# A streaming encoder step on one core: the first projection's rows are divided by their rms beforehand, and its results leave PSUM in fewer steps

## The chip, the core and the metric

The kernel runs on one core of a Trainium2 chip. TensorE (PE) multiplies matrices into PSUM, VectorE (DVE), ScalarE (ACT) and GpSimd (POOL) do the elementwise work, and SyncE (SP) issues the transfers. The metric is the device time of one execution in microseconds (us), the median of several runs. Each engine works through its own list of instructions strictly in order; that list is fixed when the program is built.

## The reference

One layer of a hybrid encoder runs over 2048 prompt rows and 32 sample rows of 1024 features. What the change touches is the first norm and the first projection, and what is made of its columns:

```python
def rmsnorm(x, g):
    y = x32 * lax.rsqrt(jnp.mean(x32 * x32, axis=-1, keepdims=True) + NORM_EPS)
    return (y * g.astype(jnp.float32)).astype(x.dtype)
...
z = RMSNorm(x) @ w_in        # q, k, v (768 columns) and the RWKV part zr (1792 columns)
z_prev = jnp.concatenate([shift_prev.astype(zr.dtype), zr[:, :-1]], axis=1)
zs = zr + (z_prev - zr) * lw['rwkv_mu']
r, k, v, wd, ad, gd = jnp.split(zs, RWKV_SPLITS, axis=-1)
```

q, k and v go to a sliding-window attention, zs to an RWKV-7 recurrence over chunks of 64 rows. Their outputs are joined and projected (w_out), a cross attention over 256 memory rows follows, then a feed-forward block with squared relu and a last norm. Besides y, the last projected row (the shift) and caches are returned.

## The kernel before

Everything is held transposed: features on the 128 partitions, rows of the sequence along the free axis. Products are made in three passes for accuracy: an operand w is split into a high part w_h and a rest w_l (ACT writes the high part, DVE or POOL subtracts for the rest), x likewise into xh and xl, and `mm3` (L230, its matmuls on lines 234, 235 and 236) adds xh w_h + xl w_h + xh w_l over eight slices of 128 features: 24 matmuls, called a group below.

The 2080 rows form four groups of rows (0 to 3) of 544, 512, 512 and 512, each cut into two blocks of 272 or 256. For group of rows g, phase Yg projects the 14 units of 128 columns that make zr, phase Zg the 6 units of q, k, v. Each unit's weights are loaded once and used for both blocks, so the groups on PE alternate between first and second block. `prep` (L264) makes a block ready: it loads x to `xb`, of which there is one buffer, writes xh (ACT, with the norm's gain as its scale) and xl (DVE, `gsplit`), and returns a function for the row norms. That function (`rms`, L193, with `sumsq`, L176) squares each slice on ACT, adds the squares on POOL (for rows 0 to 543 PE adds them instead), sums over partitions by a matmul with ones, `ps_rms` (L190), and makes 1/rms by two activations, Ln and Exp. It is called behind the first group's matmuls. So PE multiplies rows that aren't divided yet, and the division is part of the evacuation of `ps_z`: DVE multiplies by `rms_acc` from PSUM to `zo` (for q with 0.125 too). For zr there follow two steps on `zo`: ACT writes mu times `zo`, shifted by one row, to `zm`; DVE adds omu times `zo` (omu is 1 - mu) and `zm`, in place. SP then stores `zo` to zrw or zqkv in memory, from where the RWKV tiles (`zin`, L528) and the attention tiles load it. `ps_z` and `ps_rms` share two PSUM banks (`pmm`, L81); a bank is free for the next group once its reader is done. `zo` and `zm` have three buffers each, the weights two.

A list written by hand (PLAN, L35) names the phases in order: Y0 and Z0, then 17 RWKV tiles (R00 to R33 and Rs), attention tiles (A), Y1 to Z3, the output projection (O), cross attention (C, X, D), and then the feed-forward part. From it, from priorities for each kind of work (the recurrence's first, the matmuls of `mm3` last, as fillers) and from modelled durations, a scheduler fixes every engine's list. The RWKV tiles are one long chain in which each tile needs the state of the one before; groups of `mm3` fill PE in between.

Of the kernel before, what the change touches and what calls it, by code (L numbers as in the profile page):

```python
# [22 lines left out]
KC = D // P  # L23
# [27 lines left out]
def hymba_step_kernel(  # L51
# [46 lines left out]
    def pc(key, i, n=1):  # L98
        return par[:, PG[key] + i:PG[key] + i + n]
# [161 lines left out]
    def halves_of(g):  # L261
        return [(0, 272), (272, 272)] if g == 0 else [(0, 256), (256, 256)]

    def prep(src, nb, gkey, nk=KC, pe=False, alt=False):  # L264
        if alt:
            xa = [rp.tile([P, 1024], F32, tag=t, name="xa", bufs=BKB if t == "bk" else 1) for t in ("bk", "wa", "lt")]
            xs_ = []
            for j, t in enumerate(xa):
                w = min(3, nk - 3 * j)
                v = t[:, 0:w * nb].rearrange("p (a b) -> p a b", a=w)  # L270
                Q.dma_start(v, src[:, 3 * j:3 * j + w])
                xs_ += [v[:, i] for i in range(w)]

            def xk(k):
                return xs_[k]
        else:
            xb = zp.tile([P, KC, NH], F32, tag="xb", name="xb", bufs=1)
            if pe:
                for k in range(0, nk, 2):
                    Q.dma_start(xb[:, k:k + 2, 0:nb], src[:, k:k + 2])  # L280
            else:
                Q.dma_start(xb[:, 0:nk, 0:nb], src)

            def xk(k):
                return xb[:, k, 0:nb]
        xh = [zp.tile([P, XS, NH], F32R, tag="xh", name="xh", bufs=XB) for k in range(0, nk, XS)]
        xl = [zp.tile([P, XS, NH], F32R, tag="xl", name="xl", bufs=XB) for k in range(0, nk, XS)]
        if gkey is None:
            for k in range(0, nk, 2):
                a, b = divmod(k, XS)  # L290
                split(xb[:, k:k + 2, 0:nb], xh[a][:, b:b + 2, 0:nb], xl[a][:, b:b + 2, 0:nb],
                      ENG[E6] if k % 4 else V)
            return xh, xl, None
        for k in range(nk):
            a, b = divmod(k, XS)
            gsplit(xk(k), xh[a][:, b, 0:nb], xl[a][:, b, 0:nb], pc(gkey, k))
        return xh, xl, lambda: rms(zp, xk, nb, "zt", pe, 3)

    def dense(wsrc, units, xs, blks, evac, nk=KC, per=1, rs=None, fast=False):
        cols = nk * P  # L300
# [20 lines left out]
    def zphase(g, units):  # L321
        lab(f"Z{g}.prep")
        o, n = GROUPS[g]
        blks = halves_of(g)
        if g not in zst:
            def xprep(b0, nb):
                return prep(xT3[:, :, o + b0:o + b0 + nb], nb, "mix", pe=(g == 0), alt=(g == 0 and b0 > 0))

            zst[g] = ([(lambda b=b: xprep(*b)) if g == 0 and b[0] else xprep(*b) for b in blks], [None] * 2)
        xs, rs = zst[g]  # L330
        lab(f"Z{g}.mm")
        zms = {}

        def evac(ft, bi, b0, nb, ps, r):
            zo = zp.tile([P, NH], F32, tag="zo", name="zo", bufs=3)
            if ft < 4:
                stt(zo[:, 0:nb], ps[:, 0:nb], 0.125, r, MUL, MUL)
            else:
                tt(zo[:, 0:nb], ps[:, 0:nb], r, MUL)
            if ft >= 6:  # L340
                f = ft - 6
                zm = zp.tile([P, NH + 2], F32, tag="zm", name="zm", bufs=3)
                if g == 0 and bi == 0:
                    V.tensor_copy(zm[:, 0:1], zin0[:, f:f + 1])
                    V.memset(zm[:, 33:34], 0.0)
                    act(zm[:, 1:33], zo[:, 0:32], scale=mu2[:, f:f + 1])
                    act(zm[:, 34:nb + 2], zo[:, 32:nb], scale=mu2[:, f:f + 1])
                    V.tensor_copy(shs[:, f:f + 1], zo[:, 31:32])
                    stt(zo[:, 0:32], zo[:, 0:32], omu[:, f:f + 1], zm[:, 0:32], MUL, ADD)
                    stt(zo[:, 32:nb], zo[:, 32:nb], omu[:, f:f + 1], zm[:, 33:nb + 1], MUL, ADD)  # L350
                    zms[f] = zm[:, nb + 1:nb + 2]
                else:
                    V.tensor_copy(zm[:, 0:1], carry[:, f:f + 1] if bi == 0 else zms[f])
                    act(zm[:, 1:1 + nb], zo[:, 0:nb], scale=mu2[:, f:f + 1])
                    if bi == 1 and g == 3:
                        V.tensor_copy(shp[:, f:f + 1], zo[:, nb - 1:nb])
                    stt(zo[:, 0:nb], zo[:, 0:nb], omu[:, f:f + 1], zm[:, 0:nb], MUL, ADD)
                    zms[f] = zm[:, nb:nb + 1]
                if bi == 1 and g < 3:
                    V.tensor_copy(carry[:, f:f + 1], zms[f])  # L360
            Q.dma_start(zqkv[g][:, ft, b0:b0 + nb] if ft < 6 else zrw[g][:, ft - 6, b0:b0 + nb], zo[:, 0:nb])

        dense(win, units, xs, blks, evac, rs=rs, fast=(g == 0 and 0 not in units))
        if 0 in units:
            zouts(g)
        else:
            if g == 0:
                Q.dma_start(ssh, shs)
            if g == 3:
                Q.dma_start(psh, shp)  # L370
# [794 lines left out]
```

## Time and profile before

| what | us |
|---|---|
| median of three runs | 3291.79 (3285.52 to 3298.22) |
| profiled execution, its own time | 3291.38 |
| span of the profiled execution | 3289.6 |
| PE busy | 3046.8 (93%) |
| DVE busy | 1895.3 (58%) |
| ACT busy | 1247.3 (38%) |
| POOL busy | 1018.4 (31%) |

The profile is of one execution; the sums of the prediction are made against that execution's own time, 3291.38 us, of which 1.8 us lie outside the span. It stands 0.4 us below the median of the runs, far less than the runs differ among themselves (0.2% to either side). The mean clock granted to TensorE in it was 0.958. Shares over the whole span are means over stages with different limits, so the rows below are mostly of single stretches.

### The profile page before, as it was taken

The numbers are of one execution on the slowest core, as the hardware profiler recorded it, in microseconds if no ns is written. First come the engines' busy times: TensorE is split into PE (matmuls) and PEld (weight loads), VectorE is DVE, ScalarE is ACT, GpSimd is POOL, SyncE is SP. The second block draws the span as 40 slices with busy tenths as digits, with TensorE's granted clock in tenths as the row PEclk, the third lists the DMA queues.
The fourth block names the chain that finished last, engine by engine and source line by source line (L and its number), as shares of the span: only waits on it lengthen the run. The fifth ranks groups of instructions, "written<-read, shape, count | busy, mean of one in ns | idle before, by whom it ended". The sixth has DMA issues, their size and how long they took to land.

```text
span 3289.6 us, 64991 instructions
## 1 busy us (share of the span) xinstructions
PE 3046.8 (93%) x25605; PEld 2851.5 (87%) x25605; DVE 1895.3 (58%) x4482; ACT 1247.3 (38%) x2824; POOL 1018.4 (31%) x1034
## 2 busy tenths in 40 slices
PE   8988888888978998889988999999999999999998
PEld 7877766777767887778978999999999999999998
DVE  4577887876777566774334644444446654444446
ACT  5354555443454454445443312222224322222223
POOL 3543353334344343434444511111112521111111
PEclk9989988999989999989989999999999999999999
DMA  5433333323333453436766211111113211111112
GB/s 174 137 87 96 95 115 106 89 86 109 103 108 109 130 161 105 118 98 205 229 213 197 75 41 46 46 52 40 52 39 105 72 52 46 45 52 52 44 47 90
DMA packets 338660, 317.98 MB, mean 97 GB/s; under 512 B 84490, under 2 KB 260146, under 8 KB 338354
## 3 DMA queue, kind: packets, MB, share of 16 engines
q1 hardware_dynamic: 338354, 313.83, 31.1%
q8 instruction: 201, 3.29, 0.4%
q14 instruction: 105, 0.86, 0.1%
HBM read 245.21 MB, written 68.77 MB: 95 GB/s over the span
## 4 chain that ended last, share of the span: by engine, by line
PE 63%; DVE 15%; DMA 11%; ACT 4%; issue 3%; SPq 2%; POOL 1%; DVEq 0%; ACTq 0%; POOLq 0%
PE ps_up L236 7%; PE ps_dn L995 7%; PE ps_up L235 7%; PE ps_up L234 7%; PE ps_dn L997 7%; PE ps_dn L996 7%; PE ps_z L234 4%; PE ps_z L236 4%; PE ps_z L235 4%; DMA lt<-lscr 3%; DVE z L69 2%; DVE prd L69 1%; DVE xt L69 1%; DMA xscr<-xt 1%; SPq L650 1%
## 5 line engine op out<-in xcount | busy, mean ns | idle before, releaser
L234 PE MATMUL ps_z<-xh,w_h 128*128 128x256 f32 (+1 forms) x2368 | 721.7, 305 | 81.2 <-DVE zo L69 31.8
L235 PE MATMUL ps_z<-xl,w_h 128*128 128x256 f32 (+1 forms) x2368 | 711.3, 300 | 1.8 <-DVE xl L72 1.8
L236 PE MATMUL ps_z<-xh,w_l 128*128 128x256 f32 (+1 forms) x2368 | 708.2, 299 | 0.0
L66 ACT ACTIVATE w_h<-w_raw 128x512 fp32r<-128x512 f32 x576 | 345.3, 626 | 794.5 <-PE ps_up L235 258.5
L69 DVE TENSOR_TENSOR x<-ps_dn,x 128x352 f32<-128x352 f32 (+1 forms) x768 | 389.6, 516 | 365.8 <-PE ps_dn L997 362.1
L234 PEld LDWEIGHTS ps_z<-xh,w_h 128*128 128x128 f32 x2368 | 474.9, 201 | 106.5 <-DVE zo L69 27.7
L69 POOL TENSOR_TENSOR w_l<-w_raw,w_h 128x512 fp32r<-128x512 f32 x300 | 396.3, 1335 | 550.5 <-ACT w_h L66 513.4
L69 POOL TENSOR_TENSOR rl<-rl 128x352 f32<-128x352 f32 (+1 forms) x192 | 161.5, 842 | 1136.9 <-ACT uh L66 1136.9
L236 PE MATMUL ps_up<-fh,w_l 128*128 128x352 f32 (+1 forms) x1536 | 495.6, 323 | 1.3 <-DVE w_l L69 1.2
L995 PE MATMUL ps_dn<-uh,w_h 128*128 128x352 f32 (+1 forms) x1536 | 492.9, 321 | 4.1 <-DVE x L69 3.0
L996 PE MATMUL ps_dn<-ul,w_h 128*128 128x352 f32 (+1 forms) x1536 | 490.8, 320 | 4.9 <-DVE ul L69 4.9
L234 PE MATMUL ps_up<-fh,w_h 128*128 128x352 f32 (+1 forms) x1536 | 493.3, 321 | 0.4 <-DVE zo L69 0.4
L235 PE MATMUL ps_up<-fl,w_h 128*128 128x352 f32 (+1 forms) x1536 | 491.1, 320 | 0.5 <-DVE fl L72 0.5
L997 PE MATMUL ps_dn<-uh,w_l 128*128 128x352 f32 (+1 forms) x1536 | 490.5, 320 | 0.0
L235 PEld LDWEIGHTS ps_z<-xl,w_h 128*128 128x128 f32 x2368 | 474.1, 200 | 18.5 <-issue 11.0
L236 PEld LDWEIGHTS ps_z<-xh,w_l 128*128 128x128 f32 x2368 | 473.9, 200 | 13.4 <-issue 9.4
L69 DVE TENSOR_TENSOR w_l<-w_raw,w_h 128x512 fp32r<-128x512 f32 x276 | 198.4, 738 | 228.1 <-ACT w_h L66 228.0
L996 PEld LDWEIGHTS ps_dn<-ul,w_h 128*128 128x128 f32 x1536 | 289.6, 189 | 5.5 <-DVE ul L69 5.2
L995 PEld LDWEIGHTS ps_dn<-uh,w_h 128*128 128x128 f32 x1536 | 288.7, 188 | 6.1 <-DVE x L69 2.5
L236 PEld LDWEIGHTS ps_up<-fh,w_l 128*128 128x128 f32 x1536 | 288.4, 188 | 2.1 <-DVE w_l L69 1.9
L235 PEld LDWEIGHTS ps_up<-fl,w_h 128*128 128x128 f32 x1536 | 288.5, 188 | 1.1 <-DVE fl L72 0.8
L234 PEld LDWEIGHTS ps_up<-fh,w_h 128*128 128x128 f32 x1536 | 288.2, 188 | 1.2 <-DVE zo L69 0.6
(246 smaller groups left out, 4516.7 us busy)
## 6 DMA issues: line engine op xcount, KB each, us to landing
w_raw<-in_win SPq DMA_DIRECT2D x160, 256.0 KB, 3.0
w_raw<-in_wup SPq DMA_DIRECT2D x136, 256.0 KB, 2.7
w_raw<-in_wdn SPq DMA_DIRECT2D x136, 256.0 KB, 2.9
w_raw<-in_wout SPq DMA_DIRECT2D x64, 256.0 KB, 3.6
zrw<-zo SPq DMA_DIRECT2D x84, 128.0 KB, 3.4
zin<-zrw SPq DMA_DIRECT2D x16, 512.0 KB
w_raw<-in_wcq SPq DMA_DIRECT2D x32, 256.0 KB, 3.4
w_raw<-in_wco SPq DMA_DIRECT2D x32, 256.0 KB, 3.3
```

The lines of the kernel that those rows point to most:

```text
L66: S.activation(out, in_, func, **kw)
L69: (eng or V).tensor_tensor(out, a, b, op=op)
L234: T.matmul(ps, lhsT=a, rhs=c, start=(k == 0), stop=False)
L235: T.matmul(ps, lhsT=a, rhs=d, start=False, stop=False)
L236: T.matmul(ps, lhsT=b, rhs=c, start=False, stop=(k == nk - 1))
L650: Q.dma_start(lscr[8 * k:8 * k + 8].rearrange("q s t -> s q t"), ab8[r0:r0 + 16, :, x0:x0 + 16])
L995: T.matmul(ps[:, 0:n], lhsT=wh[:, ms], rhs=us[i][0], start=(i == 0), stop=False)
L996: T.matmul(ps[:, 0:n], lhsT=wh[:, ms], rhs=us[i][1], start=False, stop=False)
L997: T.matmul(ps[:, 0:n], lhsT=wl[:, ms], rhs=us[i][0], start=False, stop=(i == 1))
```

## The change

`prep` has a new argument, norm, which the first projection sets. With it the row norms are made first, and each slice of x in `xb` is multiplied in place by 1/rms before it is split: eight products for each block, 64 in all, on POOL; for rows 0 to 543 every other one on DVE. What comes out of PSUM is then the projection itself. q, k and v are copied to `zo` by ACT (q with 0.125 as the scale). For zr ACT makes `zm` from PSUM, DVE makes the sum from PSUM and `zm` in one step, and the small copies of the last rows (`shs`, `shp`) read PSUM too; the DVE multiplication from PSUM to `zo` is gone for all 160 groups.

```diff
--- before.py
+++ after.py
@@ -261,7 +261,7 @@
     def halves_of(g):
         return [(0, 272), (272, 272)] if g == 0 else [(0, 256), (256, 256)]
 
-    def prep(src, nb, gkey, nk=KC, pe=False, alt=False):
+    def prep(src, nb, gkey, nk=KC, pe=False, alt=False, norm=False):
         if alt:
             xa = [rp.tile([P, 1024], F32, tag=t, name="xa", bufs=BKB if t == "bk" else 1) for t in ("bk", "wa", "lt")]
             xs_ = []
@@ -291,10 +291,14 @@
                 split(xb[:, k:k + 2, 0:nb], xh[a][:, b:b + 2, 0:nb], xl[a][:, b:b + 2, 0:nb],
                       ENG[E6] if k % 4 else V)
             return xh, xl, None
+        if norm:
+            r = rms(zp, xk, nb, "zt", pe, 3)
         for k in range(nk):
             a, b = divmod(k, XS)
+            if norm:
+                tt(xk(k), xk(k), r, MUL, V if pe and k % 2 else G)
             gsplit(xk(k), xh[a][:, b, 0:nb], xl[a][:, b, 0:nb], pc(gkey, k))
-        return xh, xl, lambda: rms(zp, xk, nb, "zt", pe, 3)
+        return xh, xl, None if norm else lambda: rms(zp, xk, nb, "zt", pe, 3)
 
     def dense(wsrc, units, xs, blks, evac, nk=KC, per=1, rs=None, fast=False):
         cols = nk * P
@@ -324,7 +328,7 @@
         blks = halves_of(g)
         if g not in zst:
             def xprep(b0, nb):
-                return prep(xT3[:, :, o + b0:o + b0 + nb], nb, "mix", pe=(g == 0), alt=(g == 0 and b0 > 0))
+                return prep(xT3[:, :, o + b0:o + b0 + nb], nb, "mix", pe=(g == 0), alt=(g == 0 and b0 > 0), norm=True)
 
             zst[g] = ([(lambda b=b: xprep(*b)) if g == 0 and b[0] else xprep(*b) for b in blks], [None] * 2)
         xs, rs = zst[g]
@@ -333,28 +337,26 @@
 
         def evac(ft, bi, b0, nb, ps, r):
             zo = zp.tile([P, NH], F32, tag="zo", name="zo", bufs=3)
-            if ft < 4:
-                stt(zo[:, 0:nb], ps[:, 0:nb], 0.125, r, MUL, MUL)
+            if ft < 6:
+                act(zo[:, 0:nb], ps[:, 0:nb], scale=0.125 if ft < 4 else 1.0)
             else:
-                tt(zo[:, 0:nb], ps[:, 0:nb], r, MUL)
-            if ft >= 6:
                 f = ft - 6
                 zm = zp.tile([P, NH + 2], F32, tag="zm", name="zm", bufs=3)
                 if g == 0 and bi == 0:
                     V.tensor_copy(zm[:, 0:1], zin0[:, f:f + 1])
                     V.memset(zm[:, 33:34], 0.0)
-                    act(zm[:, 1:33], zo[:, 0:32], scale=mu2[:, f:f + 1])
-                    act(zm[:, 34:nb + 2], zo[:, 32:nb], scale=mu2[:, f:f + 1])
-                    V.tensor_copy(shs[:, f:f + 1], zo[:, 31:32])
-                    stt(zo[:, 0:32], zo[:, 0:32], omu[:, f:f + 1], zm[:, 0:32], MUL, ADD)
-                    stt(zo[:, 32:nb], zo[:, 32:nb], omu[:, f:f + 1], zm[:, 33:nb + 1], MUL, ADD)
+                    act(zm[:, 1:33], ps[:, 0:32], scale=mu2[:, f:f + 1])
+                    act(zm[:, 34:nb + 2], ps[:, 32:nb], scale=mu2[:, f:f + 1])
+                    V.tensor_copy(shs[:, f:f + 1], ps[:, 31:32])
+                    stt(zo[:, 0:32], ps[:, 0:32], omu[:, f:f + 1], zm[:, 0:32], MUL, ADD)
+                    stt(zo[:, 32:nb], ps[:, 32:nb], omu[:, f:f + 1], zm[:, 33:nb + 1], MUL, ADD)
                     zms[f] = zm[:, nb + 1:nb + 2]
                 else:
                     V.tensor_copy(zm[:, 0:1], carry[:, f:f + 1] if bi == 0 else zms[f])
-                    act(zm[:, 1:1 + nb], zo[:, 0:nb], scale=mu2[:, f:f + 1])
+                    act(zm[:, 1:1 + nb], ps[:, 0:nb], scale=mu2[:, f:f + 1])
                     if bi == 1 and g == 3:
-                        V.tensor_copy(shp[:, f:f + 1], zo[:, nb - 1:nb])
-                    stt(zo[:, 0:nb], zo[:, 0:nb], omu[:, f:f + 1], zm[:, 0:nb], MUL, ADD)
+                        V.tensor_copy(shp[:, f:f + 1], ps[:, nb - 1:nb])
+                    stt(zo[:, 0:nb], ps[:, 0:nb], omu[:, f:f + 1], zm[:, 0:nb], MUL, ADD)
                     zms[f] = zm[:, nb:nb + 1]
                 if bi == 1 and g < 3:
                     V.tensor_copy(carry[:, f:f + 1], zms[f])
```

The scheduler makes new lists for all engines from this. Three places of the lists follow; a row is line, operation, output and inputs.

TensorE, the end of Z0 and the start of Y1, before; pA belongs to an RWKV tile, the ps_z rows of 272 columns are Z0's and those of 256 are Y1's.

```order
L236 MATMUL ps_z<-xh,w_l 128x272
L225 MATMUL pA<-z_1841,bk 128x128
L225 MATMUL pA<-z_1842,bk 128x128
...
L234 MATMUL ps_z<-xh,w_h 128x256
L235 MATMUL ps_z<-xl,w_h 128x256
L236 MATMUL ps_z<-xh,w_l 128x256
...
L190 MATMUL ps_rms<-rms_acc,cst 128x256
```

TensorE, the same place now; pvo, pbk, pss and ppt belong to RWKV and attention tiles, whose matmuls are left out between.

```order
L236 MATMUL ps_z<-xh,w_l 128x272
L190 MATMUL ps_rms<-rms_acc,cst 128x256
L225 MATMUL pA<-z_1829,bk 128x128
...
L799 MATMUL pvo<-cst,vf 32x128
...
L228 MATMUL pbk<-cst,bk 128x128 x4
...
L581 MATMUL pss<-sq,cst 128x512
L228 MATMUL ppt<-cst,sc 128x32
...
L190 MATMUL ps_rms<-rms_acc,cst 128x256
L234 MATMUL ps_z<-xh,w_h 128x256
```

Both blocks' sums of squares now stand ahead of Y1's first group; before, Y1's first group stood right behind the RWKV tile's pA and the first sum of squares inside it.

GpSimd at the same place, before; w_l are rests of weights, rms_acc the additions of squares, z of an RWKV tile.

```order
L69 TENSOR_TENSOR w_l<-w_raw,w_h 128x512 x5
L69 TENSOR_TENSOR rms_acc<-rms_sq,rms_acc 128x256 x7
L69 TENSOR_TENSOR w_l<-w_raw,w_h 128x512 x2
L69 TENSOR_TENSOR rms_acc<-rms_sq,rms_acc 128x256 x7
L69 TENSOR_TENSOR w_l<-w_raw,w_h 128x512 x2
L69 TENSOR_TENSOR z_2315<-zin,pp 64x4x64
```

GpSimd, the same place now; xb<-xb,rms_acc are the products.

```order
L69 TENSOR_TENSOR w_l<-w_raw,w_h 128x512 x5
L69 TENSOR_TENSOR xb<-xb,rms_acc 128x256 x8
L69 TENSOR_TENSOR rms_acc<-rms_sq,rms_acc 128x256 x4
L69 TENSOR_TENSOR z_2303<-zin,pp 64x4x64
...
L69 TENSOR_TENSOR rms_acc<-rms_sq,rms_acc 128x256 x3
...
L69 TENSOR_TENSOR bk<-kka,cs 64x8x64 x2
L69 TENSOR_TENSOR xb<-xb,rms_acc 128x256 x8
L571 MEMSET pp 128x8
```

The first block's eight products stand ahead of the second block's additions of squares, and RWKV operations (z, bk) have moved in between.

TensorE at the start of Y2, before; pvar, pgate, po and ppt belong to RWKV and attention tiles, and Y2's groups go on between them.

```order
L235 MATMUL ps_z<-xl,w_h 128x256
L236 MATMUL ps_z<-xh,w_l 128x256
L228 MATMUL ppt<-cst,sc 128x128 x2
L190 MATMUL ps_rms<-rms_acc,cst 128x256
L772 MATMUL pvar<-yq,cst 128x512
L225 MATMUL pgate<-sg,g_70 128x128 x4
L225 MATMUL po<-pT,vt 64x128 x4
L228 MATMUL ppt<-cst,sc 128x128 x4
L234 MATMUL ps_z<-xh,w_h 128x256
```

TensorE at the start of Y2 now; pvx is the last of the memory projection, pS, py, pvar and pgate are of an RWKV tile, pvo and po of attention tiles.

```order
L399 MATMUL pvx<-cst,zov 128x128
L190 MATMUL ps_rms<-rms_acc,cst 128x256
...
L225 MATMUL pS<-uv,bkt 64x64 x7
...
L774 MATMUL pvar<-yq,cst 128x512
L225 MATMUL pgate<-sg,g_70 128x128 x4
...
L799 MATMUL pvo<-cst,vf 128x128
...
L190 MATMUL ps_rms<-rms_acc,cst 128x256
L234 MATMUL ps_z<-xh,w_h 128x256
```

Before, Y2's groups stood on both sides of the sum of squares; now no group of Y2 stands until both sums are through, with most of an RWKV tile between them.

## Rows read from the trace of the kernel before

**Rows 1.** Windows: stretch, length, busy PE, PEld, DVE, ACT, POOL, clock, DMA share, GB/s.

```profile
31.00:131.00 100.00, 99.33 (x788) 98.17 (x787) 51.47 (x157) 45.89 (x98) 46.06 (x39) 1.00 0.46 142
206.00:450.00 244.00, 216.60 (x2581) 182.75 (x2581) 195.04 (x556) 117.59 (x296) 92.11 (x86) 0.92 0.33 92
560.00:820.00 260.00, 228.61 (x2849) 196.74 (x2849) 193.94 (x522) 117.47 (x263) 100.22 (x91) 0.93 0.33 95
1020.00:1184.00 164.00, 156.23 (x1625) 140.37 (x1626) 93.88 (x307) 77.61 (x191) 57.03 (x54) 0.98 0.41 123
1810.00:3290.00 1480.00, 1463.18 (x9200) 1456.60 (x9200) 727.27 (x1336) 379.99 (x766) 275.74 (x310) 1.00 0.17 55
```

**Rows 2.** Chain that ended last by line, 560 to 820 us, then 1020 to 1184 us.

```profile
by line: DMA lt<-lscr 8.3%; issue 7.5%; DVE z L69 6.2%; SPq L650 4.0%; PE ps_z L234 3.6%; DMA xscr<-xt 3.6%; DVE tm L696 3.6%; PE ps_z L236 3.4%; PE ps_z L235 3.4%; DVE zo L72 3.1%; DVE yb L72 3.1%; DVE prd L69 3.0%; DVE xt L69 2.9%; PE pA
by line: PE ps_z L235 17.1%; PE ps_z L234 17.1%; PE ps_z L236 16.7%; DMA xb<-mscr 4.2%; DMA lt<-lscr 3.6%; PE pq L225 3.5%; issue 2.7%; SPq L671 2.6%; PE ppt L228 2.5%; PE po L225 2.5%; PE xpo L498 1.8%; DMA vx<-in_cmv 1.6%; PE pW L225 1.4%
```

**Rows 3.** Groups of instructions by form: busy us, mean ns of one, idle before, releaser.

```profile
L69 DVE TENSOR_TENSOR zo<-ps_z,rms_acc 128x256 f32<-128x256 f32 x96 | 39.7, 414 | 19.5 <-PE ps_z L236 18.1 <-DMA w_raw<-in_win 0.9 <-ACT rms_acc L66 0.2
L72 DVE SCALAR_TENSOR_TENSOR zo<-zo,omu,zm 128x256 f32<-128x256 f32 x84 | 55.5, 661 | 24.5 <-ACT zm L66 24.1
L72 DVE SCALAR_TENSOR_TENSOR xl<-xb,par,xh 128x256 fp32r<-128x256 f32 x104 | 60.5, 622 | 34.2 <-ACT xh L66 34.1
L66 ACT ACTIVATE zm<-zo,mu 128x256 f32<-128x256 f32 x84 | 42.4, 504 | 77.8 <-DVE zo L69 77.1
L66 ACT ACTIVATE ao<-po 128x256 f32<-128x256 f32 x32 | 12.0, 375 | 10.2 <-PE po L225 10.0
L69 POOL TENSOR_TENSOR rms_acc<-rms_sq,rms_acc 128x256 f32<-128x256 f32 x98 | 77.5, 791 | 99.2 <-ACT rms_sq L66 86.8 <-ACT rms_acc L66 6.7 <-ACT sm L66 2.0
```

**Rows 4.** Timeline of ACT and DVE in Y0: start, us, instruction, idle before it.

```profile
63.60 1.21 ACT L66 ACTIVATE w_h<-w_raw 128x512 fp32r<-128x512 f32 x2 [1.29 <-PE ps_z L235]
63.68 0.44 DVE L69 TENSOR_TENSOR zo<-ps_z,rms_acc 128x272 f32<-128x272 f32 x1 [0.74 <-PE ps_z L236]
64.72 0.51 ACT L66 ACTIVATE zm<-zo,mu 128x272 f32<-128x272 f32 x1
65.26 0.64 DVE L72 SCALAR_TENSOR_TENSOR zo<-zo,omu,zm 128x272 f32<-128x272 f32 x1 [1.14 <-ACT zm L66]
66.70 0.44 DVE L69 TENSOR_TENSOR zo<-ps_z,rms_acc 128x272 f32<-128x272 f32 x1 [0.74 <-PE ps_z L236]
```

**Rows 5.** Waits of PE from 131 to 206 us: total, times, longest.

```profile
PE ps_z L234 <- DVE zo L72: 6.0, 1, 6.0
```

**Rows 6.** Start of Y1: a piece of the chain, then timelines of ACT and PE.

```profile
159.10 5.37 DMA xb<-in_xT
164.49 3.31 ACT L66 ACTIVATE xh<-xb,par 128x256 fp32r<-128x256 f32 x8 [2.04 <-DMA xb<-in_xT]
163.53 0.60 PE L190 MATMUL ps_rms<-rms_acc,cst 128*128 128x256 f32 x2
169.54 0.47 ACT L66 ACTIVATE rms_acc<-ps_rms,eps_t 128x256 f32<-128x256 f32 x1
170.38 0.40 ACT L66 ACTIVATE rms_acc<-rms_acc 128x256 f32<-128x256 f32 x1
```

**Rows 7.** Windows of PE's ps_z matmuls at three starts: length, busy, clock, DMA, GB/s.

```profile
161.00:182.00 21.00, 9.33 (x51) 0.84 0.56 175
544.00:564.00 20.00, 11.62 (x72) 0.91 0.44 128
1013.00:1033.00 20.00, 3.71 (x21) 0.91 0.38 120
```

**Rows 8.** Windows of the tile zo: length, busy DVE, busy ACT, clock, DMA, GB/s.

```profile
206.00:450.00 244.00, 29.88 (x57) 11.57 (x23) 0.92 0.33 92
560.00:820.00 260.00, 32.59 (x66) 13.61 (x27) 0.93 0.33 95
```

**Rows 9.** Timeline of PE near the start of the program.

```profile
26.19 1.98 PE L163 MATMUL pb<-gat,anti 128*128 128x512 f32 x4 [0.39 <-DMA gat<-vd]
```

## The prediction

> **What bounds the kernel now.** I read windows first, since shares of the whole span mix stages. In the feed-forward part, from 1810 us on, PE is busy 1463 of 1480 us, and in Y0, from 31 to 131, 99.33 of 100 [rows 1]: there PE is the bound, and work taken from DVE buys nothing as long as a result leaves its bank in time. Between, in 206 to 450 and 560 to 820, PE is busy 217 of 244 and 229 of 260, and DVE 195 and 194 [rows 1]: neither is full. The chain of waits says why: from 560 to 820 it is led by a transfer inside the RWKV tiles, DVE lines and small matmuls, with each line of the projection's matmuls at 3.4 to 3.6%; from 1020 to 1184 those three lines hold 51% [rows 2]. So the first stretches are ruled by the recurrence with the projection as filler, the second by PE. What the change can gain lies in the first kind, what it can lose is time in which PE has no group to run.
>
> **What it removes.** 112 multiplications of zr from PSUM at 0.41 us, and the mix's second input moves from SBUF to PSUM [rows 3]. The trace has no mix from PSUM. Bounds: 0.41 us, the two-input DVE operation from PSUM of that shape, and 0.66, the mix as it is [rows 3]; I take 0.42, since the multiplication by 1/rms has the same operands, one in PSUM and one in SBUF. Then a zr group costs DVE 0.42 instead of 1.07, which is 61% less. The Trainium skill, page "SBUF — State Buffer", section "Who interferes with whom", says that a DVE instruction with two SBUF inputs contends with a GpSimd instruction that reads SBUF, and one with at most one SBUF input doesn't; the two means of the one shape, 661 and 414 ns, agree [rows 3], and without the rule the mix would be priced the same.
>
> In 206 to 450 and 560 to 820 DVE spends 29.9 and 32.6 us on `zo` [rows 8], so some 38 us of DVE work go. Only what stands on the chain counts: the mixes are 3.1% of 260 us, 8.1 us [rows 2], of which 37% goes, 3 us. The multiplications aren't in the list, whose last whole entries stand at 2.9%, so they are below 7.5 us. The relief is 3 to 10.5 us in that window and, with about as much `zo` work in the other, 6 to 21 in both; nothing, if a later group of matmuls rather than DVE is what the recurrence waits for. I take **−8** (0 to −21).
>
> q, k and v, 48 groups, move from 0.41 us of DVE to ACT at 0.375, the copy from PSUM of that shape [rows 3]; ACT is busy under half of these windows [rows 1], which hides it. One place gains: in Z0, PE waited 6.0 us for a DVE evacuation of q behind RWKV work [rows 5]. ACT's list is not behind that work: **−6** (0 if ACT is as late).
>
> **What it costs in the steady state.** In Y0 groups follow each other at 3.02 us (63.68 to 66.70), and DVE frees a bank 0.44 us after the group's end [rows 4]. Now the bank is held until `zm` and the mix are through: behind the two weight splits of 1.21 us, 0.51 and some 0.42, about 2.1 us after the end. That is under 3.02, with two banks, so I cost it at **nothing**; the cover is 0.9 us, and where ACT is later than that PE stalls by the difference. The 8 products done by DVE are those of rows 0 to 543, ahead of a window in which DVE is half idle [rows 1].
>
> **What it adds: the starts of Y1, Y2 and Y3.** Before, a block could be multiplied as soon as it was split, with 1/rms needed only behind its first group. Now the norm stands ahead, and the lists put *both* blocks' `ps_rms` ahead of the first group. With one `xb` the steps are in series. For the first block: `ps_rms` 0.3, Ln 0.47, Exp 0.40 [rows 6], eight products on POOL at 0.79 (bounds: POOL's addition of the same shape; nothing shorter on POOL in these rows), 6.3, the last xh 0.41: 7.9 us. Then `xb` is free and the second block comes: load 5.4 [rows 6], first square 0.4, seven additions on POOL at 0.79 [rows 3], 5.5: 11.3. Together some 19 to 20 us from the first `ps_rms` to the second.
>
> In such a stretch before ran groups of the next Y: PE was busy with ps_z for 9.33, 11.62 and 3.71 us in windows of 20 us at the three starts [rows 7]. That work is displaced, 24.7 us. How much is lost? At least 0, if all of it later fills idle time of PE, which is 27 and 31 us in the two long windows [rows 1]; at most 24.7. The stretches after these starts are ruled by the recurrence, but its next tiles can't take the rows before Y2's or Y3's groups are done, so I take the whole: **+24.7**.
>
> Behind that the second block's first group runs at the pace of its products: slice k can be multiplied only when product k is done, 8 × 0.79 = 6.3 instead of 3.0 us: 3 × 3.3 = **+9.9** (0 if recurrence matmuls fill it). At the program's start the norms stand ahead as well; but PE's stream doesn't begin before the bias matmuls behind a transfer at 26.19 [rows 9], after the norms' own time. **0** (−6 to +5).
>
> Sum: 24.7 + 9.9 − 6 − 8 = +20.6; 3291.4 + 20.6 = **3312 us**. The profiled execution is 0.4 us below the median of the runs, so the same holds for that.
>
> **The rivals.** About 0.5%, 16 us, is what a measurement of this kernel can tell from no change.
>
> *Given back.* The displaced groups are the recurrence's filler. Without them in its way a tile's matmuls run sooner, and the groups fill later gaps. For: PE idles 27 and 31 us in the two windows [rows 1], more than the 24.7 displaced. Against: Y3 lies in a stretch where PE is busy 156 of 164 [rows 1], and R20 stands behind all of Y2 in the new lists. Then of +34.6 about 14 remain, and the sum is 0: 3291, between 3285 and 3300.
>
> *DVE was the limit (the other side).* The recurrence's chain passes through many DVE lines [rows 2], and DVE is busy 80% and 75% there [rows 1]; 38 us less in its queue may shorten waits that the chain's list puts down to others. Then the bubbles at the starts lie under the recurrence, which decides, and the relief is around 15 of its bound of 21: 3291.4 − 15 − 6 = 3270. It decides from the point at which the next RWKV tile isn't waiting for the Y before it. Against: R20 does wait for Y2.
>
> *Products against splits.* The products are POOL operations with two SBUF inputs, each followed by an xl on DVE with two SBUF inputs. If the two can't overlap, each product waits for an xl, of 0.41 (as from PSUM) to 0.62 us [rows 3]: 8 × 0.41 = 3.3 to 5.0 us a block, over six blocks +20 to +30, 3332 to 3342. For: the mix with two SBUF inputs takes 661 ns where the shape needs 414, so such waits exist [rows 3]. Against: `xl` at 622 shows them at two thirds already, and RWKV work lies between. The rule of the Trainium skill's section named above would make this an exclusive lock.
>
> *The bank is late.* That the later release of the bank stalls PE in Y0 is not a case of its own: at 0.5 us for each of its 28 groups it would be 14 us, which lies in the ranges above.
>
> **How the numbers follow.** The forecast, bubbles lost for the most part, has 0.42 and a range of its own of 3300 to 3330; a quarter of it lies within the bound. Given back 0.22, nearly all within. DVE was the limit 0.24, mostly faster by more than the bound. Products against splits 0.12, slower. Slower: 0.32 + 0.12 = 0.44. Same: 0.10 + 0.19 + 0.02 = 0.31. Faster: 0.03 + 0.22 = 0.25. The range is 3266 to 3344: it leaves out the lower part of the DVE case, at its bound of −27 (3264), and what lies above the upper product case, together under 2 in 10; it holds the bound of the unknown costs on the other side, 24.7 + 9.9 + 5 (3331).
>
> **What would show it.** In the trace of after: at the start of Y1, Y2 and Y3 two `ps_rms` some 20 us apart with no ps_z matmul of that Y between, and PE idle or with RWKV work alone; products of 0.79 us on POOL, longer if they collide with splits; the mix at 0.42 us; Z0's wait of 6.0 us gone; Y0's groups still at 3.02 us. If RWKV tiles from R00 to R13 are done much earlier and the end of stage one (1810 us) is earlier too, the DVE case is right. If the stage ends as before though the gaps are there, the groups were given back. The prediction is wrong above all if PE waits in the steady state for the bank, which I cost at nothing, or if RWKV tiles become shorter by more than 1 us each.

## The result and the profile after

The changed kernel takes 3340.69 us (median of four runs, 3335.33 to 3342.62), the kernel before in the same runs 3289.73: a ratio of 1.0157, with a 95% interval of 1.0141 to 1.0174, or 51 us more. The profiled execution took 3335.33 with a span of 3333.4, so 44 us more than that of before; it is the fastest of the four, hence 44 and not 51.

The first two lines of the page of after: span, and for each engine busy time, share and instructions.

```profile
span 3333.4 us, 64922 instructions
PE 3063.5 (92%) x25605; PEld 2861.5 (86%) x25605; DVE 1835.1 (55%) x4330; ACT 1259.5 (38%) x2872; POOL 1064.8 (32%) x1090
```

DVE lost 60 us of work, as it should. PE has the same 25605 matmuls, but they are busy 16.7 us longer (3063.5 against 3046.8), and PE stands idle 269.9 us instead of 242.8 (span less busy): +27.1. These two make the 43.8 us of the span.

Groups of after by form, for [rows 3]:

```profile
L72 DVE SCALAR_TENSOR_TENSOR zo<-ps_z,omu,zm 128x256 f32<-128x256 f32 x84 | 39.9, 476 | 41.2 <-ACT zm L66 40.7
L66 ACT ACTIVATE zm<-ps_z,mu 128x256 f32<-128x256 f32 x84 | 39.1, 467 | 29.0 <-PE ps_z L236 28.5
L66 ACT ACTIVATE zo<-ps_z 128x256 f32<-128x256 f32 x36 | 13.3, 372 | 8.8 <-PE ps_z L236 8.3 <-ACT ab L66 0.5
L69 POOL TENSOR_TENSOR xb<-xb,rms_acc 128x256 f32<-128x256 f32 x48 | 38.2, 833 | 5.9 <-ACT rms_acc L66 5.5 <-POOL z L69 0.4
L72 DVE SCALAR_TENSOR_TENSOR xl<-xb,par,xh 128x256 fp32r<-128x256 f32 x104 | 64.5, 656 | 19.2 <-ACT xh L66 18.9 <-POOL rms_acc L69 0.2
```

The prices were near: the mix 0.476 us (taken: 0.42), the copy 0.372 (0.375), the product 0.833 (0.79). The split xl went from 0.622 to 0.656.

PE at the starts of Y1 and Y2, its timeline (for [rows 6]; what stands between is recurrence and attention work):

```profile
175.16 0.29 PE L236 MATMUL ps_z<-xh,w_l 128*128 128x272 f32 x1
175.29 0.59 PE L190 MATMUL ps_rms<-rms_acc,cst 128*128 128x256 f32 x2
...
212.65 1.22 PE L190 MATMUL ps_rms<-rms_acc,cst 128*128 128x256 f32 x2
213.31 0.78 PE L234 MATMUL ps_z<-xh,w_h 128*128 128x256 f32 x1
...
576.16 1.06 PE L190 MATMUL ps_rms<-rms_acc,cst 128*128 128x256 f32 x2
...
612.09 1.22 PE L190 MATMUL ps_rms<-rms_acc,cst 128*128 128x256 f32 x2
612.75 0.78 PE L234 MATMUL ps_z<-xh,w_h 128*128 128x256 f32 x1
```

No group of the projection runs between: 37.4 and 35.9 us from the first sum to the second, not 19 to 20. I call the time from the end of the last ps_z matmul of a phase to the start of the next phase's first the gap. Before, the gaps at Y1, Y2 and Y3 are 1.0, 4.6 and 0 us; after, 37.9, 43.5 and 32.9.

Where the 37.4 us go is seen in the timelines of ACT, POOL and DVE at Y1 in after:

```profile
178.02 0.63 ACT L66 ACTIVATE w_h<-w_raw 128x512 fp32r<-128x512 f32 x1 [1.98 <-DMA w_raw<-in_win]
...
178.84 0.47 ACT L66 ACTIVATE rms_acc<-ps_rms,eps_t 128x256 f32<-128x256 f32 x1
...
179.95 5.91 POOL L69 TENSOR_TENSOR xb<-xb,rms_acc 128x256 f32<-128x256 f32 x8
...
191.91 0.18 DVE L69 TENSOR_TENSOR prd<-xt,lt 128x15 f32<-128x15 f32 x1 [4.26 <-DMA lt<-lscr]
...
193.07 0.48 DVE L72 SCALAR_TENSOR_TENSOR xl<-xb,par,xh 128x256 fp32r<-128x256 f32 x1
...
194.79 0.46 DVE L72 SCALAR_TENSOR_TENSOR xl<-xb,par,xh 128x256 fp32r<-128x256 f32 x1
...
200.72 0.42 ACT L66 ACTIVATE rms_acc<-xb 128x256 f32<-128x256 f32 x1 [0.65 <-DMA xb<-in_xT]
...
207.49 1.44 POOL L69 TENSOR_TENSOR z<-zin,pp 64x256 f32<-64x256 f32 x2 [2.05 <-ACT pp L66]
...
211.48 0.72 POOL L69 TENSOR_TENSOR rms_acc<-rms_sq,rms_acc 128x256 f32<-128x256 f32 x1 [0.94 <-ACT rms_sq L66]
```

The products (5.9 us) and the load (5.4, from 195.3 to 200.7) are as priced. But Ln stands 3 us late behind Z0's last weight split, itself waiting for a transfer; the last xl ends at 195.25, 9.4 us after the last product, 4.26 us of it because a recurrence step ahead of it on DVE waits for its own transfer; and squares and additions take 11.5 us instead of 5.9, with recurrence work of ACT and POOL between. These three, 3.0, 9.0 and 5.6 us above their estimates, are 17.6 of the 18 us that the estimate lacks.

PE at the start of the program, first before,

```profile
9.04 0.59 PE L234 MATMUL ps_z<-xh,w_h 128*128 128x272 f32 x1 [9.04 <-ACT w_h L66]
```

and PE and ACT in after, with two pieces of the chain of waits:

```profile
13.28 1.25 PE L181 MATMUL ps_rms<-rms_acc,cst 128*128 128x272 f32 x2 [13.28 <-DMA cst<-in_cst]
...
17.64 4.33 PE L186 MATMUL ps_rms<-rms_sq,cst 128*128 128x272 f32 x10
...
24.84 0.60 PE L234 MATMUL ps_z<-xh,w_h 128*128 128x272 f32 x1 [2.86 <-ACT xh L66]
...
35.44 1.98 PE L163 MATMUL pb<-gat,anti 128*128 128x512 f32 x4 [1.21 <-DMA gat<-vd]
...
37.95 0.48 ACT L66 ACTIVATE rms_acc<-ps_rms,eps_t 128x272 f32<-128x272 f32 x1
...
26.36 3.82 DVE xl L72 x8
30.19 5.20 DMA gat<-vd
```

The first group starts at 24.84 instead of 9.04: the sums wait until 13.28 for the transfer of the ones (`cst`), which the first group didn't need before, and end at 21.97. The bias matmuls stand at 35.44 instead of 26.19 [rows 9]. Their input `gat` (L156) lies in the one buffer of `xb`, so its transfer goes out at 30.19, once the last split of the first block is done (30.18). The first store to zrw is issued at 34.8 (before 23.5), the second at 52.0 (35.1); from there 26 more take 80.0 us, before 80.1. The steady state of Y0 costs nothing, as forecast (from the end of its 5th group to that of its 28th 69.6 us before, 69.7 after); the start costs 17 us, and the recurrence's first tile begins at 148.6 instead of 131.2 (its first pss matmul).

Windows of before and of after behind the gap at Y1 (columns as in [rows 1]), first before:

```profile
150.00:300.00 150.00, 130.28 (x1425) 112.54 (x1424) 114.60 (x346) 79.07 (x207) 61.37 (x58) 0.93 0.35 99
```

and after, with the two long windows and a stretch ahead of R20:

```profile
150.00:300.00 150.00, 114.17 (x1234) 94.92 (x1233) 109.28 (x309) 77.84 (x208) 78.37 (x81) 0.80 0.31 83
206.00:450.00 244.00, 215.37 (x2504) 184.35 (x2504) 178.58 (x543) 123.28 (x312) 102.13 (x101) 0.88 0.31 86
560.00:820.00 260.00, 225.41 (x2760) 192.86 (x2749) 178.69 (x503) 127.17 (x299) 104.78 (x102) 0.91 0.33 96
690.00:820.00 130.00, 120.20 (x1499) 108.08 (x1498) 70.37 (x201) 56.01 (x122) 48.19 (x44) 0.95 0.35 105
```

PE is not only idle more in 150 to 300; the granted clock is 0.80 there instead of 0.93. And ahead of R20 the chain of waits has turned into the projection (690 to 820 us, first before, then after):

```profile
by line: DMA lt<-lscr 8.4%; issue 7.7%; DVE z L69 6.0%; SPq L650 5.8%; PE ps_z L234 4.6%; PE ps_z L235 4.2%; PE ps_z L236 4.2%; DVE prd L69 3.5%; DVE xt L69 3.3%; PE pA L225 3.2%; DVE tm L696 3.2%; DVE yb L72 3.1%; DMA xscr<-xt 2.6%; ACT wa
by line: PE ps_z L234 15.5%; PE ps_z L236 15.1%; PE ps_z L235 15.0%; DMA lt<-lscr 4.5%; PE py L225 3.8%; DVE z L69 2.7%; PE pA L225 2.5%; DMA w_raw<-in_win 2.5%; SPq L673 2.4%; DVE kka L69 2.3%; PE pS L225 2.0%; DVE prd L69 2.0%; DVE xt L69
```

The projection's three lines are 46% of it, before 13%. R13 begins at 691.1 us (before 706.8), in spite of the later start; R20 then begins at 816.5 (before 778.2), 19 us behind the last store of Y2 (797.4; before 741.3). From there on the tiles lag by 27 to 45 us.

### The profile page after: what moved, and what is told of

It is laid out like the page before. It is cut to its first block, busy times and chain, and to the rows that moved or that the text cites. A ratio compares the mean times of both kernels' runs of the same rounds, so it can differ in the third digit from the quotient of the medians.

```text
span 3333.4 us, 64922 instructions
## 1 busy us (share of the span) xinstructions
PE 3063.5 (92%) x25605; PEld 2861.5 (86%) x25605; DVE 1835.1 (55%) x4330; ACT 1259.5 (38%) x2872; POOL 1064.8 (32%) x1090
## 4 chain that ended last, share of the span: by engine, by line
PE 63%; DVE 15%; DMA 10%; ACT 5%; issue 3%; SPq 3%; POOL 1%; DVEq 0%; POOLq 0%; ACTq 0%
PE ps_dn L997 7%; PE ps_up L236 7%; PE ps_dn L998 7%; PE ps_dn L999 7%; PE ps_up L234 7%; PE ps_up L235 7%; PE ps_z L234 5%; PE ps_z L236 4%; PE ps_z L235 4%; DMA lt<-lscr 2%; DVE z L69 2%; DMA xb<-x2scr 1%; DVE xl L72 1%; DVE prd L69 1%; SPq L652 1%
```

## The experiments

Each is built from one of the two kernels, so its lists are made anew. Differences are against the kernel before in the same runs; the gaps are those at Y1, Y2, Y3; gaps, busy and idle of PE are of the profiled execution, which in after, e13 and e14 took 5 to 8 us less than the run's median and in e3 and e16 6 to 7 us more.

| run | us | ratio to before, 95% | difference | gaps, us | PE busy, idle |
|---|---|---|---|---|---|
| before | 3289.73 | 1 | 0 | 1.0, 4.6, 0 | 3046.8, 242.8 |
| after | 3340.69 | 1.0157 (1.0141 to 1.0174) | +51.0 | 37.9, 43.5, 32.9 | 3063.5, 269.9 |
| e1_evac_only | 3275.52 | 0.9950 (0.9935 to 0.9965) | -16.5 | 0, 6.0, 0 | 3041.5, 232.6 |
| e2_norm_only | 3356.69 | 1.0202 (1.0187 to 1.0217) | +64.7 | 37.9, 43.7, 24.4 | 3065.9, 288.6 |
| e3_rows0 | 3336.39 | 1.0137 (1.0121 to 1.0152) | +44.4 | 0, 2.2, 0 | 3069.9, 271.5 |
| e4_rows123 | 3318.64 | 1.0085 (1.0068 to 1.0102) | +26.6 | 37.2, 42.8, 23.2 | 3053.1, 261.6 |
| e5_fold | 3308.53 | 1.0037 (1.0026 to 1.0049) | +14.0 | 0.7, 5.3, 0 | 3055.5, 248.4 |
| e6_two_xb | 3283.70 | 0.9966 (0.9951 to 0.9980) | -10.8 | 6.6, 9.1, 23.6 | 3038.4, 245.8 |
| e7_not_rows2 | 3327.77 | 1.0090 (1.0069 to 1.0110) | +33.3 | 35.7, 2.6, 30.9 | 3063.0, 263.6 |
| e8_control | 3292.11 | 0.9987 (0.9974 to 1.0001) | -2.4 | 1.4, 3.8, 0 | 3047.5, 241.4 |
| e9_before_two_xb | 3302.94 | 1.0022 (1.0009 to 1.0036) | +9.5 | 1.3, 1.8, 0 | 3044.4, 258.0 |
| e10_rows123_two_xb | 3271.52 | 0.9944 (0.9924 to 0.9963) | -21.9 | 19.4, 16.8, 2.4 | 3036.9, 233.0 |
| e11_prio | 3353.73 | 1.0180 (1.0160 to 1.0200) | +60.3 | 37.6, 51.2, 24.8 | 3067.6, 285.7 |
| e12_rows123_two_xb_prio | 3328.20 | 1.0109 (1.0094 to 1.0124) | +34.8 | 18.4, 12.4, 15.3 | 3063.6, 260.7 |
| e13_norm_early | 3291.23 | 0.9983 (0.9973 to 0.9992) | -4.9 | 2.3, 16.5, 29.4 | 3043.4, 238.4 |
| e14_products_shared | 3289.38 | 0.9986 (0.9975 to 0.9996) | -6.7 | 18.4, 9.9, 19.3 | 3033.8, 248.0 |
| e15_control2 | 3295.66 | 1.0012 (1.0000 to 1.0024) | +2.9 | 1.0, 4.7, 1.5 | 3045.7, 247.8 |
| e16_control3 | 3299.00 | 1.0021 (1.0009 to 1.0033) | +6.3 | 1.2, 3.2, 0 | 3048.3, 254.7 |

**The two halves apart: e1_evac_only and e2_norm_only.** Theory: the evacuation gains, the norms ahead of the products cost; the rival has it the other way round.

```diff
 e1: prep(..., norm=False); evacuation of the change, 1/rms not used
 e2: prep(..., norm=True); evacuation of before, with
-                tt(zo[:, 0:nb], ps[:, 0:nb], r, MUL)
+                V.tensor_copy(zo[:, 0:nb], ps[:, 0:nb])
```

> Left out: the division by the rms; the norms are still computed where the kernel before has them, but nothing reads them. q, k, v are copied by ACT and the mix is made from PSUM, as in the change. Theory 1 (the loss is all in making the norms ahead of the products, the evacuation part gains): faster than before, 3265 to 3285 us, tiles R00 to R13 some 4 us shorter each as in the changed kernel, Y0's 28 stores within 92 us of each other as before. Theory 2 (the evacuation itself costs, since the bank is held until the mix is through): slower than before by 10 us or more, and Y0's stores spread over 97 us as in the changed kernel.

> Same results as the reference. Rows are divided ahead of the products as in the change, but the evacuation is the old one: DVE copies PSUM to zo, ACT makes zm from zo, DVE mixes. Theory 1: slower than the changed kernel, since it has the cost and not the gain: 3345 to 3370 us, with gaps of 35 to 50 us between the last store of Z0, M, C0 and the first of Y1, Y2, Y3. Theory 2 (evacuation costs): 3295 to 3320 us.

e1 is 16.5 us faster than before, e2 64.7 slower: the theory holds and the rival falls. e2 less after is 13.7, so the evacuation is worth 14 to 17 us either way, and the norms ahead cost 65 to 68 (64.7, and 51.0 + 16.5). Two details of the expectation were wrong. Y0's 28 stores lie 96.9 us apart in e1 (before 91.8), which was to be the rival's sign; but the last goes at 114.5 (before 115.2), and it is the first that is sooner (17.7 against 23.5). And the eight tiles from the first to R13 take 566.0 us in e1 and 575.6 before, 1.2 less each, not 4. In after they take 542.5, but 574.0 in e2, whose gaps at Y1 and Y2 are the same: so it isn't the missing groups of the projection alone that make them shorter in after, and what does is not shown.

**The start and the three other starts: e3_rows0 and e4_rows123.**

```diff
+ norm=g in (0,)   and the evacuation of the change for g in (0,)      (e3)
+ norm=g in (1, 2, 3)   and the evacuation of the change for those     (e4)
```

> Same results as the reference. Only group of rows 0 (Y0, Z0) has the change, groups 1 to 3 are as before. Theory 1a (the late start of the program, 17 us at the end of Y0, is carried to the end): +10 to +20 us against before. Theory 1b (the recurrence makes it good before it has to wait for a later Y): within 8 us of before.

> Same results as the reference. Only groups of rows 1 to 3 have the change, group 0 is as before. Theory 1a (the start is carried to the end): +25 to +35 us against before, the rest of the +51. Theory 1b (only the starts of Y1 to Y3 count): +40 to +55, as the whole change.

e4 came as the first theory had it: without the change in rows 0 to 543, 24.4 us of the 51 are gone (51.0 - 26.6). But it is not the recurrence that carries the start to the end in after. R12 and R13 begin at 623.5 and 691.1 there, at 623.4 and 689.5 in e4: by then it has made the late start good. The projection has not: Y2's last store goes at 797.4 against 777.4, and R20, behind it, begins at 816.5 against 793.0. e3 fits neither theory: +44.4 with next to no gap at Y1 to Y3. Its recurrence begins 16.5 us late (147.7), as in after, and is 5.7 late two tiles on but 34 late at R13 (740.5); Y2 is through by then (737.4). PE is busy 23.1 us longer than before, in an execution that took 6.8 us more than the run's median. More is lost behind the start, which the other runs don't show; why stays open. The two shares don't add up (71.0 against 51.0).

**Another way to the same gain: e5_fold.**

```diff
-                tt(zo[:, 0:nb], ps[:, 0:nb], r, MUL)
+                stt(zo[:, 0:nb], ps[:, 0:nb], omu[:, f:f + 1], r, MUL, MUL)
...
-                    act(zm[:, 1:1 + nb], zo[:, 0:nb], scale=mu2[:, f:f + 1])
-                    stt(zo[:, 0:nb], zo[:, 0:nb], omu[:, f:f + 1], zm[:, 0:nb], MUL, ADD)
+                    act(zm[:, 1:1 + nb], zo[:, 0:nb], scale=rat[:, f:f + 1])
+                    tt(zo[:, 0:nb], zo[:, 0:nb], zm[:, 0:nb], ADD, G)
```

> Same results as the reference. Rows are not divided beforehand. DVE multiplies PSUM by omu and 1/rms in one step to zo, ACT makes zm from zo with the scale mu/omu, and POOL adds zm to zo; q, k, v as before. So DVE loses the mix (0.66 us a group) without any norm ahead of a product. Theory 1 (the gain is DVE time of the recurrence's stretches, the loss the norms ahead): faster than before, 3270 to 3285 us. Theory 2 (work moved to POOL delays the recurrence's own POOL steps and takes the gain back): 3290 to 3310.

The time is that of the second theory. POOL's waits in this kernel from 206 to 450 us (total, times, longest) bear it out:

```profile
POOL zo L69 <- ACT zm L66: 38.1, 9, 7.8
```

POOL stands 38 us with the addition at its head, and what the list has behind it, the recurrence's POOL work too, can't pass. How much of the 14 us this is was not told apart.

**The second buffer: e6_two_xb, e9_before_two_xb, e10_rows123_two_xb.**

```diff
-            xb = zp.tile([P, KC, NH], F32, tag="xb", name="xb", bufs=1)
+            xb = zp.tile([P, KC, NH], F32, tag="xb", name="xb", bufs=2)
```

> The whole change with two xb buffers instead of one, so that the second block's load, squares and sum need not wait for the first block's products and splits. Theory 1 (the two blocks' steps in series make the gaps of 45, 49 and 42 us between stores at the starts of Y1, Y2, Y3): gaps of 25 us or less, 3305 to 3325 us. Theory 2 (the gaps come from splits and products queued behind recurrence work on ACT, DVE and POOL, whatever the buffers): gaps of 35 us and more, 3330 to 3345 us.

> The kernel before with two xb buffers, nothing else. Theory 1 (the second buffer takes away what the change put in series, which the kernel before does not have): within 8 us of before, 3284 to 3300 us. Rival (a second buffer helps the output projection and cross attention as much, so the 57 us that it gave the changed kernel are not about the norms): 3240 to 3270 us.

> Same results as the reference. Groups of rows 1 to 3 changed, group 0 as before, two xb buffers. Theory 1 (the late start of 17 us is carried by the recurrence to the end): 10 to 20 us less than with all four groups changed and two buffers, 3263 to 3275 us. Rival (the start is made good by then): 3278 to 3290 us.

The second buffer is worth 62 us to the whole change (51.0 to -10.8) and 48 to e4's (26.6 to -21.9), and nothing to the kernel before, which gets 9.5 us slower (3 us beyond what was expected of it). So what it takes away came with the change, as the series of the two blocks' steps did, and is not something that the kernel had anyway. It gave far more than I expected of it. From the last store of a phase to the first of the next e6 has 21.6, 27.8 and 32.2 us, after 45.8, 49.0 and 42.4: the series, and also queues. In e6 `gat` no longer waits for `xb`: its transfer goes out at 20.68 and the bias matmuls stand at 29.38, yet the recurrence's first tile begins at 150.1, later than in after. So the late start hangs on the norms and not on the bias. e10 came as its first theory had it, 11 us less than e6 and the fastest of all: PE and POOL at the start of its Y1,

```profile
165.07 0.70 PE L190 MATMUL ps_rms<-rms_acc,cst 128*128 128x256 f32 x2
...
182.76 1.22 PE L190 MATMUL ps_rms<-rms_acc,cst 128*128 128x256 f32 x2
183.42 0.78 PE L234 MATMUL ps_z<-xh,w_h 128*128 128x256 f32 x1
...
167.32 6.16 POOL L69 TENSOR_TENSOR xb<-xb,rms_acc 128x256 f32<-128x256 f32 x8
173.44 1.52 POOL L69 TENSOR_TENSOR rms_acc<-rms_sq,rms_acc 128x256 f32<-128x256 f32 x2
```

show that the second block's additions follow the products at once, without the load and the splits between; 17.7 us from sum to sum instead of 37.4.

**One gap less: e7_not_rows2.**

```diff
+ norm=g in (0, 1, 3)   and the evacuation of the change for those
```

> Same results as the reference. Groups of rows 0, 1 and 3 have the change, group 2 (Y2, Z2) is as before. Theory 1 (R20 waits for all of Y2, so the late Y2 sets the recurrence back by some 40 us): the recurrence tile of R20 begins 25 to 40 us earlier than in the changed kernel, and the time is 3300 to 3320 us. Theory 2 (the start of the program is what is carried to the end, and the wait for Y2 stands for time that would be lost anyway): 3330 to 3345 us.

Y2's gap is gone (2.6 us), but R20 begins at 813.1 us, 3 earlier than in after, not 25 to 40, and the time lies between the two theories' ranges. Y2's own gap does not set R20's start: its first group starts at 608.6 us, only 4.2 sooner, because the memory projection ahead of it now ends 36.7 us later (606.0 against 569.3; why is not shown). What counts is how far the whole stream of the projection has come: Y2's last store goes at 795.4, in after at 797.4.

**The order of the queues: e11_prio, e12_rows123_two_xb_prio, e14_products_shared, e13_norm_early.**

```diff
+            old = setp("s")                       (e11, e12: ahead of the norm; setp(old) behind the splits)
-                tt(xk(k), xk(k), r, MUL, V if pe and k % 2 else G)
+                tt(xk(k), xk(k), r, MUL, V if k % 2 else G)                     (e14)
-PLAN = """Y0 B Z0 ...
+PLAN = """Y0 B N1 Z0 ...       N1: Y1's loads, norms and products               (e13)
```

> The whole change with one xb buffer; the norms, products and splits ahead of Y0 to Y3 have the recurrence's priority in the scheduler instead of a lower one. Theory 1 (of the gaps' 42 to 49 us only some 20 are the series of steps, the rest is recurrence work in the queues ahead of them): gaps of 20 to 32 us at Y1, Y2, Y3 and 3305 to 3330 us. Theory 2 (the gap is the series of steps and the one buffer alone): gaps of 40 us and more, 3333 to 3350 us.

> Same results as the reference. Groups 1 to 3 changed, group 0 as before, two xb buffers, and the recurrence's priority for the norms, products and splits. Theory 1 (both matter): shorter gaps than with two buffers alone (22 to 32 us), and 3255 to 3270 us. Rival (splits that go before the recurrence's own steps delay it by as much): the same as without the priority or up to 15 us more.

> Same results as the reference. Groups 1 to 3 changed, group 0 as before, two xb buffers; of each block's eight products four are on DVE and four on POOL, as for rows 0 to 543, instead of all on POOL. Theory 1 (the products' 6 us on POOL stand in the series ahead of each start): gaps 3 to 6 us shorter at each of Y1, Y2, Y3 and 3256 to 3268 us. Rival (products on DVE stand in the way of the recurrence's DVE steps, and splits and products have the same engine): 3270 to 3285 us.

> Same results as the reference. Groups 1 to 3 changed, group 0 as before, two xb buffers, and in the program's order Y1's loads, norms and products (not its splits) stand ahead of Z0, in both buffers. Theory 1 (a gap at a start costs as PE's idle time and as a lower clock behind it, and the recurrence carries it on): the gap at Y1 is under 20 us instead of 37, the granted clock from 150 to 300 us is 0.90 or more, and the time is 8 to 20 us below that of the same kernel without it, 3252 to 3264 us. Theory 2 (the recurrence, not the projection, decides until R13, so the gap at Y1 is covered): 3266 to 3276 us.

The priority left e11's gap at Y1 as it was, lengthened Y2's and shortened Y3's, and the time is above both theories' ranges; so it did not take the recurrence's work out of the way, and what the queues alone would give was not told apart. In e12 it kept e10's gap at Y1, shortened Y2's, lengthened Y3's by 13 us and cost 57 us more, far beyond both theories; a wait of PE from 560 to 820 us that is 0.2 us in e10,

```profile
PE ps_z L235 <- DVE xl L72: 8.5, 3, 3.6
```

is a part of it. So short gaps at the first two starts alone don't make the time. In e14 four products on DVE shorten the gap at Y2 and lengthen that at Y3, and it is 15 us slower than e10: the rival, some 4 us beyond its range. e13 removes Y1's gap, and the granted clock from 150 to 300 us is 0.93 as before (e10: 0.85); but its norm's sum now stands ahead of Z0:

```profile
132.11 1.22 PE L190 MATMUL ps_rms<-rms_acc,cst 128*128 128x256 f32 x2 [9.75 <-POOL rms_acc L69]
```

PE waits for it, a new gap of 19.1 us stands between Y0 and Z0, and the time is 17 us worse against before than e10's; both theories' times are missed.

**What an order alone does: e8_control, e15_control2, e16_control3.**

```diff
-  V.tensor_copy(shs[:, f:f + 1], zo[:, 31:32])                                      (e8)
+  G.tensor_copy(shs[:, f:f + 1], zo[:, 31:32])
-  V.tensor_copy(zm[:, 0:1], carry[:, f:f + 1] if bi == 0 else zms[f])               (e15)
+  G.tensor_copy(zm[:, 0:1], carry[:, f:f + 1] if bi == 0 else zms[f])
-  V.tensor_copy(carry[:, f:f + 1], zms[f])                                          (e16)
+  act(carry[:, f:f + 1], zms[f])
```

> The kernel before with 14 copies of one column (the shift of the sample rows) moved from DVE to POOL: next to no work, but all lists are made anew. It prices what another order alone does. Theory 1 (differences of 15 us and more between these kernels are due to what was changed in them): within 8 us of before. Rival (the order is that sensitive): 10 us or more to either side, and then single terms below that can't be told from it.

> The kernel before with 98 copies of one column (the first column of zm) moved from DVE to POOL: next to no work, but the lists of all engines come out differently from there on. It prices what another order alone does. If orders matter little: within 8 us of before. If they matter as much as the unexplained part of the run with only rows 0 to 543 changed (some 25 us): 10 to 30 us to either side.

> The kernel before with 42 copies of one column (the carry) moved from DVE to ACT: again next to no work and other lists. If orders matter little: within 8 us of before. If they matter: 10 to 30 us to either side, and not the same amount as with the other control.

In e8 TensorE's list came out all but the same, so it told little. In the other two the lists differ widely, single tiles move by up to 23 us against before, and the end by 3 and 6; e9, which also changes no work, moves tiles by up to 27 and the end by 9.5. Terms of 15 us and more between these kernels are thus not the order's doing as far as these three show; smaller ones can't be told from it, and three lists don't rule it out for the larger ones that no other run explains (e3, e12).

## Why the prediction was right or wrong

The direction was right and the time lies in the wide range, but not in the forecast's own (3300 to 3330): +20.6 us were forecast, +51 measured. Two terms of the sum failed, the start of the program, put at nothing, and the series of steps at Y1 to Y3, priced at half its length.

- **The start of the program** is the step that failed most: "**0** (-6 to +5)", since PE's stream seemed not to begin before the bias matmuls at 26.19. The line was misread. Before, PE starts on Y0 at 9.04, and two of its 28 groups are done by 24.43, ahead of those matmuls; with the norms in front these two have to wait as well (the first runs from 24.84). Nor are the bias matmuls a fixed point, as their input waits for `xb`: they moved to 35.44. It is 17 us at the recurrence's first tile and 24 at the end (after less e4).
- **The starts of Y1 to Y3** had the right mechanism, both sums ahead of the first group with one buffer, shown by e6 and e10 against e9. The series was priced as if its engines had nothing else to do, 19 to 20 us where it is 36 to 37. The term was 34.6 us with the second block's pace; measured are some 40 to 43, if gains and losses add up (e4's 26.6 and e1's 16.5, of which 1 to 3 may be group 0's). That it is so near is in part luck. From the same points, the kernel before runs 44.5 us of ps_z matmuls in the 114.3 us that the gaps of after take, not 24.7; taken as lost in full, with the 9.9 for the pace, that would be 54. So a series priced too short and a loss taken as complete cancel in part. The pace itself was not told apart.
- **The relief** came out in its sum, -14 us (-8 for DVE's time and -6 for Z0), against 16.5 (e1) and 13.7 (e2 less after). Its parts did not: the wait of 6.0 us in Z0 [rows 5] is not among PE's waits of after from 131 to 216 us, but from the end of Y0's last group to that of Z0's last it takes 46.4 us there, 48.2 in e1 and 49.3 before, 1 to 3 us less and not 6.
- **DVE was the limit** was near with its relief (21 us at its point, e1 has 16.5), but the gaps don't lie under the recurrence: R20 waits for Y2.
- **Given back.** R13 begins 16 us sooner than before in after, as this rival has it, but 12 later in e2 (718.9) with the same gaps at Y1 and Y2. And the projection then has to be caught up with: R20 waits, as the prediction said of the new lists.
- **The clock** was no term of the sum. Of the span's 43.8 us, 16.7 are the same matmuls busy longer; where the gap at Y1 lies the granted clock is 0.80 instead of 0.93, and e13, without that gap, has 0.93. That all of the 16.7 is the clock's isn't shown: e10 has the mean clock of before (0.959 and 0.958) and 9.9 us less busy time.
- **Products against splits** gave 3332 to 3342 us, and that the time lies there is chance. Products take 833 ns where the additions take 761 in the same trace, and xl went from 622 to 656, far from an alternation of the two at 0.41 us a product. The rule of the Trainium skill's page "SBUF — State Buffer", section "Who interferes with whom", agrees with these means in its sign. **The late bank** did not occur.

Open stay the other 27 us of e3, why a priority costs 57, and whether queues or buffer would have shortened the gap more.

## What to carry to other kernels

A step put ahead of the first product is priced in the queues that it will stand in: here a series of 19 us took 37, because other work with its own waits lies between on engines that work in order. If a buffer makes two blocks' steps serial, give it a second copy before giving up the idea: e10, the change for rows 544 to 2079 with two xb buffers, is at 0.9944 of the kernel before (0.9924 to 0.9963), 22 us where the relief alone gave 16.5. Split the difference between two profiles into busy and idle time of the bounding engine; a gap that another stream fills can still cost clock, and it sets the one stream back that the other must later wait for.

## What the runs showed of the hardware

A DVE operation of 128x256 with two tensors, one in PSUM, took 413 ns with a constant as its scalar and 474 with a scalar for each partition, both in e5:

```profile
L72 DVE SCALAR_TENSOR_TENSOR zo<-ps_z,omu,rms_acc 128x256 f32<-128x256 f32 x84 | 39.8, 474 | 36.2 <-PE ps_z L240 33.3 <-DMA zrw<-zo 1.5 <-ACT rms_acc L66 1.3
L72 DVE SCALAR_TENSOR_TENSOR zo<-ps_z,rms_acc 128x256 f32<-128x256 f32 x24 | 9.9, 413 | 1.5 <-issue 1.0 <-PE ps_z L240 0.4
```

That is as much as lies between the 0.42 taken for the mix and the 0.476 measured. The 661 ns of the mix with both tensors in SBUF [rows 3] are a mean over two kinds: half of its 84 took 485 ns or less and the longest 1587; from PSUM the median is 478 and the longest 488. So what the mix gained was the end of the long ones, not a faster pace of the others. ACT's `zm` from PSUM took 467 ns, from SBUF 504 [rows 3].
